# A transformer layer in split float32: the order of additions and splits inside a seven-product pair

## The chip, the cores and the metric

The kernel runs on one core of a Trainium2 chip. The metric is the device time of one execution in microseconds (us), the median of several runs.

## What is computed

One layer works on x of 256 tokens by 2048 channels, all float32, with a norm before and after each part:

```
x = x + 0.5 * rms_norm(swiglu(rms_norm(x), W1_gate_up, W1_down))      # FFN 1, 2048 -> 2 x 5632 -> 2048
p = rms_norm(x) @ W_in                                                 # 2048 -> 6656
y_h = hgrn2 recurrence, forward and backward, 8 heads; y_a = attention, window 128, 8 heads
x = x + rms_norm(concat(y_h, y_a) @ W_out)                             # 2048 -> 2048
x = x + 0.5 * rms_norm(swiglu(rms_norm(x), W2_gate_up, W2_down))      # FFN 2, as FFN 1
```

Nearly all of the work is the products with the weights, 400 MB of which pass once.

## The kernel before

**Split products.** Every float32 matrix is written as h + l: h is the value rounded to the matmul's short float format, l the rest. A product is three matmuls: h with h, h with l, l with h. `split_act` makes the two parts: ScalarE copies the source into h (line 188), and VectorE subtracts h from the source into l (line 189). `split_half(raw, i)` does this for half i of a weight tile `raw` (128 partitions by 2048), so 1024 columns at a time. The weights come from DRAM into `raw` tiles by loads that the SyncE queue (SP) issues in order (line 164); there are three such tiles, for a time a fourth (`raw3`, or `rooms`, the place of X while X is not needed). The h and l tiles come from two pools of five each; a new split waits until TensorE has read the split five before.

**Pairs.** `Blocks` runs a product over pairs u of 128-row blocks of the contraction (256 rows). A plain pair takes 8 products (24 matmuls, `plain`). A seven-product pair (`seven`) takes 7 products (21 matmuls) by a scheme of Strassen's kind: the weight tile has four blocks b11, b12, b21, b22 of 512 columns, and sums of blocks are multiplied with sums of the left side. It needs four kinds of right sides:

- b11 as loaded: a split of 512 columns (`h, l`);
- the lower blocks b21 and b22 as loaded: `lower`, a split of the tile's second half;
- b11 and b22 each plus b12, written over b11 and b12 by one addition of 1024 columns (line 477): `upper`, a split of the first half;
- b22 plus the new b11 (line 481) and b21 plus that (line 483), written over b22 and b21: `last`, a second split of the second half.

So the additions of lines 481 and 483 overwrite what `lower` reads, and the last one must be done before `last`. The seven products are issued in the order b11, `lower` (two), `upper` (two), `last` (two).

**Stages.** `Gated` computes gate and up: 11 groups (g) of 512 columns, each over 8 pairs, of which pairs 1, 3 and 5 are seven-product ones from group 2 on (3 and 5 in group 1, none in group 0). `Pairs` computes the two down projections (11 of 22 pairs by seven products) and the output projection (2 of 8), in two halves of 1024 columns each. At a group's end `fold` (lines 520 to 528) adds the extra products, `units` applies silu and scale (lines 944 and 945), transposes, splits and sums (lines 400 to 404).

**The order of the work.** What each engine runs is in program order on that engine, but the program's order is not the order of the code: outside of stretches marked as manual a scheduler puts every engine's instructions in order by its own estimate of when they will be ready. So a change in the code's order can move instructions on all engines, or be undone.

Of the kernel before, what the change touches and what calls it, by code (L numbers as in the profile page):

```python
# [17 lines left out]
ALU = mybir.AluOpType  # L18
# [19 lines left out]
def hymba_layer_kernel(  # L38
# [25 lines left out]
    nc = tc.nc  # L64
# [11 lines left out]
    def nm(s):  # L76
        uid[0] += 1
        return f"{s}_{uid[0]}"

    def pa():  # L80
        return psum.tile([P, 512], F32, tag="pa", name=nm("pa"))

    def pb():
        return psum.tile([P, 512], F32, tag="pb", name=nm("pb"))
# [59 lines left out]
    def new_raw():  # L144

        raw_places.append(raw_places.pop(0))
        return raw_places[-1]

    def load(src, between=None):
        raw = new_raw()  # L150
        if len(src.shape) == 4:

            dst = raw.rearrange("p (a n b) -> p a n b", a=src.shape[1], n=src.shape[2])
            parts = [(dst[:, a], src[:, a]) for a in range(src.shape[1])]
        else:
            n = src.shape[1]
            dst = raw.rearrange("p (a b) -> p a b", a=n)
            parts = [(dst, src)]
            if n == 2:
                parts = [(dst[:, a], src[:, a]) for a in range(2)]  # L160
        for i, (to, of) in enumerate(parts):
            if i and between:
                between()
            nc.sync.dma_start(to, of)
        return raw
# [14 lines left out]
    def split_half(raw, i, hp=hip, lp=lop):  # L180
        part = raw[:, i * 1024 : (i + 1) * 1024]
        h = hp.tile([P, 1024], F32R, tag="h", name=nm("h"))
        l = lp.tile([P, 1024], F32R, tag="l", name=nm("l"))
        split_act(h, l, part)
        return h, l

    def split_act(hi, lo, src):
        nc.scalar.copy(hi, src)  # L188
        nc.vector.tensor_tensor(lo, src, hi.bitcast(F32), ALU.subtract)  # L189
# [217 lines left out]
    class Blocks:  # L407
# [58 lines left out]
        def seven(self, u, aside=None):  # L466

            self.left_early(u)
            raw = load(self.source(u))
            if aside:  # L470
                aside()
            b11, b12, b21, b22 = (raw[:, i * 512 : (i + 1) * 512] for i in range(4))
            four = raw.rearrange("p (i c) -> p i c", i=4)
            h, l = self.one_block()
            split_act(h, l, b11)

            nc.vector.tensor_tensor(  # L477
                four[:, 0:2], four[:, 0::3], four[:, 1:2].to_broadcast([P, 2, 512]), ALU.add
            )
            lower = split_half(raw, 1)  # L480
            nc.vector.tensor_tensor(b22, b11, b22, ALU.add)  # L481
            upper = split_half(raw, 0)
            nc.vector.tensor_tensor(b21, b22, b21, ALU.add)  # L483
            if aside:
                aside()
            last = split_half(raw, 1)
            if not self.p:
                self.p = [pa(), pa(), pb(), pb()]
            a, w = self.tiles[u], self.left_sums(u)

            def lhs(k, m):
                return [a[:, k, i, m * P : (m + 1) * P] for i in range(2)]

            def summed(j):
                return [w[:, j, i, :] for i in range(2)]

            def rhs(two, n):
                return [x[:, n * 512 : (n + 1) * 512] for x in two]

            for at, left, right in (  # L500
                (("p", 0), lhs(0, 0), (h, l)),
                (("c", 0, 0), lhs(1, 0), rhs(lower, 0)),
                (("c", 0, 1), summed(S4), rhs(lower, 1)),
                (("p", 1), summed(S1), rhs(upper, 0)),
                (("p", 3), summed(S3), rhs(upper, 1)),
                (("p", 2), summed(S2), rhs(last, 1)),
                (("c", 1, 0), lhs(1, 1), rhs(last, 0)),
            ):
                self.three(at, *left, *right)
# [523 lines left out]
    with tc.manual_schedule():  # L1033
# [9 lines left out]
        raw = new_raw()  # L1043
# [561 lines left out]
```

## Time and profile before

| | us |
|---|---|
| median of 3 runs (lowest, highest) | 1855.11 (1854.1, 1856.63) |
| the profiled execution | 1852.71 |
| its span, first to last instruction | 1850.9 |

| engine | busy us | share |
|---|---|---|
| TensorE matmul (PE) | 1831.9 | 99% |
| TensorE weight load (PEld) | 1516.0 | 82% |
| VectorE (DVE) | 1633.6 | 88% |
| ScalarE (ACT) | 1087.2 | 59% |

The granted TensorE clock is 0.999 of full speed on the mean. Weight loads run beside matmuls, and matmuls overlap, so the busy time of TensorE says little on how densely it works; the starts of its instructions do. In rows of the timeline the first number is the start, the second the time taken, both in us; x2 is two instructions merged; a bracket is idle time of the engine ahead of the row and what ended it. In rows of the waits, the total comes first, then how often, then the longest.

### The profile page before, as it was taken

What the parts mean: (1) busy time and instruction counts of PE and PEld (TensorE: products, weight loads), DVE (VectorE), ACT (ScalarE), POOL (GpSimd) and SP (SyncE); (2) the same over time, 40 slices, a digit from 0 to 9 for tenths busy, and PEclk for the clock granted to TensorE, in tenths of its full rate; (3) what the DMA queues carried; (4) which work ended last, traced back from release to release, by engine and by line L of the source; (5) the groups of instructions that cost most, each with busy time, mean ns of one, the idle gap of its engine ahead of it and who ended that gap; (6) DMA issues with size and microseconds to landing.
All of it is one profiled execution on the core that took longest, in us unless ns stands there. A gap on an engine that the chain in (4) does not pass through costs nothing.

```text
span 1850.9 us, 23980 instructions
## 1 busy us (share of the span) xinstructions
PE 1831.9 (99%) x8604; PEld 1516.0 (82%) x8604; DVE 1633.6 (88%) x2076; ACT 1087.2 (59%) x1465; POOL 33.3 (2%) x61
## 2 busy tenths in 40 slices
PE   9999999999999999999999999999999999999998
PEld 7888888888887787888888887888888888888786
DVE  7999999999999998577787798899999999999997
ACT  6555555555655556577677565555555555555563
POOL 1000000000000000000000000000000000000000
PEclk9999999999999999999999999999999999999999
DMA  8566666666877776655565565666666666687774
GB/s 286 191 221 214 205 194 204 206 207 202 291 267 266 242 242 209 217 177 158 168 186 165 182 215 184 205 216 209 211 202 215 219 217 205 218 282 273 242 268 172
DMA packets 192056, 400.45 MB, mean 216 GB/s; under 512 B 11976, under 2 KB 59168, under 8 KB 191168
## 3 DMA queue, kind: packets, MB, share of 16 engines
q1 hardware_dynamic: 188416, 387.24, 63.9%
q0 software_dynamic: 3520, 11.67, 1.6%
q8 instruction: 67, 1.10, 0.2%
q14 instruction: 53, 0.43, 0.1%
HBM read 383.12 MB, written 15.75 MB: 215 GB/s over the span
## 4 chain that ended last, share of the span: by engine, by line
PE 80%; DVE 10%; issue 4%; ACT 3%; DMA 3%; SPq 0%; POOL 0%; ACTq 0%; DVEq 0%; POOLq 0%
PE pa L444 33%; PE pb L444 30%; PE pa L319 8%; DVE l L189 5%; PE pa L324 4%; ACT h L188 2%; DMA raw<-in_w_mix_out_dram 1%; DMA raw<-in_w_ffn_gate_up_dram 1%; PE pa L374 1%; PE pa L373 1%; PE pa L372 1%; DVE raw L477 1%; DVE raw L481 1%; ACT xt L239 0%; PE pa L956 0%
## 5 line engine op out<-in xcount | busy, mean ns | idle before, releaser
L188 ACT CAST h<-raw 128x1024 fp32r<-128x1024 f32 (+1 forms) x691 | 676.8, 1013 | 489.7 <-DVE raw L483 179.2
L189 DVE TENSOR_TENSOR l<-raw,h 128x1024 fp32r<-128x1024 f32 (+1 forms) x691 | 794.4, 1173 | 116.5 <-ACT h L188 83.4
L444 PE MATMUL pa<-h,xt 128*128 128x512 f32 x1176 | 408.7, 393 | 1.5
L444 PE MATMUL pb<-h,xt 128*128 128x512 f32 x1060 | 370.1, 390 | 0.0
L444 PEld LDWEIGHTS pa<-h,xt 128*128 128x128 f32 x1176 | 220.0, 188 | 51.4 <-ACT h L188 7.4
L444 PEld LDWEIGHTS pb<-h,xt 128*128 128x128 f32 x1060 | 198.9, 188 | 42.2 <-DVE pb L528 0.7
L444 PE MATMUL pa<-l,xt 128*128 128x512 f32 x588 | 229.7, 391 | 0.7 <-DVE l L189 0.7
L444 PE MATMUL pb<-l,xt 128*128 128x512 f32 x530 | 206.5, 390 | 0.0
L188 ACT CAST h<-rooms 128x1024 fp32r<-128x1024 f32 x138 | 142.1, 1050 | 57.2 <-DVE rooms L483 40.8
L189 DVE TENSOR_TENSOR l<-rooms,h 128x1024 fp32r<-128x1024 f32 x138 | 165.8, 1219 | 5.3 <-ACT h L188 5.0
L319 PE MATMUL pa<-xt,h 128*128 128x512 f32 x672 | 164.7, 394 | 0.0
L444 PE MATMUL pa<-h,ht 128*128 128x512 f32 x440 | 156.1, 391 | 1.1 <-DVE pa L522 0.9
L444 PE MATMUL pb<-h,ht 128*128 128x512 f32 x440 | 155.8, 390 | 0.2 <-DVE pb L526 0.2
L319 PEld LDWEIGHTS pa<-xt,h 128*128 128x128 f32 x672 | 123.0, 188 | 23.6
L444 PEld LDWEIGHTS pa<-l,xt 128*128 128x128 f32 x588 | 110.5, 188 | 24.8 <-DVE l L189 2.3
L444 PEld LDWEIGHTS pb<-l,xt 128*128 128x128 f32 x530 | 99.5, 188 | 20.6
L477 DVE TENSOR_TENSOR raw<-raw 128x1024 f32<-128x1024 f32 x92 | 112.1, 1218 | 0.4
L444 PEld LDWEIGHTS pa<-h,ht 128*128 128x128 f32 x440 | 82.6, 188 | 20.1 <-DVE pa L525 1.6
L444 PEld LDWEIGHTS pb<-h,ht 128*128 128x128 f32 x440 | 82.6, 188 | 18.2 <-DVE pb L526 1.1
L324 PE MATMUL pa<-xt,l 128*128 128x256 f32 x672 | 91.8, 286 | 0.0
L324 PEld LDWEIGHTS pa<-xt,l 128*128 128x128 f32 x672 | 87.1, 191 | 3.2
L444 PE MATMUL pa<-l,ht 128*128 128x512 f32 x220 | 85.7, 390 | 0.0
(280 smaller groups left out, 2474.4 us busy)
## 6 DMA issues: line engine op xcount, KB each, us to landing
raw<-in_w_ffn_gate_up_dram SPq DMA_DIRECT2D x270, 512.0 KB, 4.9
raw<-in_w_ffn_down_dram SPq DMA_DIRECT2D x132, 512.0 KB, 5.3
raw<-in_w_mix_in_dram SPq DMA_DIRECT2D x52, 1024.0 KB, 5.1
rooms<-in_w_ffn_gate_up_dram SPq DMA_DIRECT2D x80, 512.0 KB, 5.4
rooms<-in_w_ffn_down_dram SPq DMA_DIRECT2D x44, 512.0 KB, 5.1
sp<-ss SPq DMA_DIRECT2D x44, 512.0 KB, 6.5
raw<-in_w_mix_out_dram SPq DMA_DIRECT2D x32, 512.0 KB, 4.8
ss<-rooms POOLq DMA_DIRECT2D x22, 512.0 KB, 5.3
```

What stands on the lines that cost most here:

```text
L188: nc.scalar.copy(hi, src)
L189: nc.vector.tensor_tensor(lo, src, hi.bitcast(F32), ALU.subtract)
L319: nc.tensor.matmul(slot[f], weights(hs, kk, f), xcol(xt, k), start=(k == 0), stop=(k == KT - 1))
L324: nc.tensor.matmul(slot[f][:, 0:T], weights(ls, kk, f), xcol(xt, kh * 8 + kk, 0), start=False, stop=False,)
L372: nc.tensor.matmul(dst, xh, h[:, o : o + n], start=(k == 0), stop=False)
L373: nc.tensor.matmul(dst, xh, l[:, o : o + n], start=False, stop=False)
L374: nc.tensor.matmul(dst, xl, h[:, o : o + n], start=False, stop=(k == KT - 1))
L444: nc.tensor.matmul(self.bank(at), lhs, rhs, start=(n == 1), stop=n in (ends, self.of[at]), skip_group_check=n > ends,)
L477: nc.vector.tensor_tensor(four[:, 0:2], four[:, 0::3], four[:, 1:2].to_broadcast([P, 2, 512]), ALU.add)
L481: nc.vector.tensor_tensor(b22, b11, b22, ALU.add)
```

## The change

In `seven`, the split of the lower blocks as loaded now comes first, directly behind that of b11; then the three additions follow each other; then the other two splits. Nothing is added or removed. The lines behind it move up by one: the three additions are on lines 477, 480 and 481 in the changed kernel.

```
             h, l = self.one_block()
             split_act(h, l, b11)
-
+            lower = split_half(raw, 1)
             nc.vector.tensor_tensor(
                 four[:, 0:2], four[:, 0::3], four[:, 1:2].to_broadcast([P, 2, 512]), ALU.add
             )
-            lower = split_half(raw, 1)
             nc.vector.tensor_tensor(b22, b11, b22, ALU.add)
+            nc.vector.tensor_tensor(b21, b22, b21, ALU.add)
             upper = split_half(raw, 0)
-            nc.vector.tensor_tensor(b21, b22, b21, ALU.add)
             if aside:
                 aside()
             last = split_half(raw, 1)
```

What the scheduler makes of it is not one order for all pairs. In a gate/up group the first seven-product pair keeps the order of before (line 477, both splits, the two other additions, the last split), and the third had the new order before the change already. The second one changes, in groups 2 to 9 of both FFNs; so does the first one of group 1 in the first FFN, and two pairs at the middle of each down projection. On VectorE, in group 3 of the first FFN (groups 4 to 9 read the same), before; the first row is the l of b11, raw_114 the weight tile, l_1452, l_1457 and l_1462 are `lower`, `upper` and `last`, l_1489 the next plain pair's first:

```order
L189 TENSOR_TENSOR l_1447<-raw_114,h_1446 128x512
L189 TENSOR_TENSOR rooms_495<-rooms_495 128x4x128
L477 TENSOR_TENSOR raw_114<-raw_114 128x1024
L189 TENSOR_TENSOR l_1452<-raw_114,h_1451 128x1024
L189 TENSOR_TENSOR l_1457<-raw_114,h_1456 128x1024
L481 TENSOR_TENSOR raw_114<-raw_114 128x512
L483 TENSOR_TENSOR raw_114<-raw_114 128x512
L189 TENSOR_TENSOR l_1462<-raw_114,h_1461 128x1024
L189 TENSOR_TENSOR l_1489<-raw_112,h_1488 128x1024
```

The same place in the changed kernel, where `lower`, `upper` and `last` are l_1451, l_1458 and l_1462:

```order
L189 TENSOR_TENSOR l_1447<-raw_114,h_1446 128x512
L189 TENSOR_TENSOR l_1451<-raw_114,h_1450 128x1024
L189 TENSOR_TENSOR rooms_495<-rooms_495 128x4x128
L477 TENSOR_TENSOR raw_114<-raw_114 128x1024
L480 TENSOR_TENSOR raw_114<-raw_114 128x512
L481 TENSOR_TENSOR raw_114<-raw_114 128x512
L189 TENSOR_TENSOR l_1458<-raw_114,h_1457 128x1024
L189 TENSOR_TENSOR l_1462<-raw_114,h_1461 128x1024
L189 TENSOR_TENSOR l_1489<-raw_112,h_1488 128x1024
```

The split of `lower` moved ahead of line 477, that of `upper` behind the three additions, next to `last`. Ahead of these rows, the first split of the plain pair from the spare room moved from behind line 400 to in front of it, and on ScalarE its h moved ahead of the copy of line 964.

On TensorE at the end of the same pair, before; h_1461 and l_1462 are `last`, h_1488 and l_1489 the next plain pair's:

```order
L444 MATMUL pb_1387<-h_1461,xs_521 128x512
L444 MATMUL pb_1304<-h_1461,xt_126 128x512
L444 MATMUL pa_1302<-h_1488,xt_127 128x512
L444 MATMUL pa_1303<-h_1488,xt_127 128x512
L444 MATMUL pb_1387<-l_1462,xs_521 128x512
L444 MATMUL pb_1387<-h_1461,xs_521 128x512
L444 MATMUL pb_1304<-l_1462,xt_126 128x512
```

And in the changed kernel:

```order
L444 MATMUL pb_1387<-h_1461,xs_521 128x512
L444 MATMUL pb_1387<-l_1462,xs_521 128x512
L444 MATMUL pb_1387<-h_1461,xs_521 128x512
L444 MATMUL pb_1304<-h_1461,xt_126 128x512
L444 MATMUL pb_1304<-l_1462,xt_126 128x512
L444 MATMUL pb_1304<-h_1461,xt_126 128x512
L444 MATMUL pa_1302<-h_1488,xt_127 128x512
```

The matmuls with h, which had been put ahead of those with l_1462, went back behind them: each product's three matmuls now stand together.

In the output projection, VectorE at the first seven-product pair, before (raw_112 is the weight tile, l_9094 and l_9099 are `lower` and `upper`; ya, g, ot and yh belong to the heads that are being finished):

```order
L477 TENSOR_TENSOR raw_112<-raw_112 128x1024
L189 TENSOR_TENSOR ya_8996<-pb_8991,ya_8996 128x2x256
L189 TENSOR_TENSOR l_9094<-raw_112,h_9093 128x1024
L1381 TENSOR_TENSOR g_8977<-g_8977,sg_8983 128x512
L481 TENSOR_TENSOR raw_112<-raw_112 128x512
L1384 SCALAR_TENSOR_TENSOR ot_8697<-ot_8697,cols,g_8977 128x256 x2
L189 TENSOR_TENSOR l_9099<-raw_112,h_9098 128x1024
L189 TENSOR_TENSOR yh_8988<-ot_8697,yh_8988 128x2x256
L483 TENSOR_TENSOR raw_112<-raw_112 128x512
```

And in the changed kernel, `lower` and `upper` being l_9093 and l_9100:

```order
L189 TENSOR_TENSOR l_9093<-raw_112,h_9092 128x1024
L189 TENSOR_TENSOR ya_8996<-pb_8991,ya_8996 128x2x256
L477 TENSOR_TENSOR raw_112<-raw_112 128x1024
L1380 TENSOR_TENSOR g_8977<-g_8977,sg_8983 128x512
L480 TENSOR_TENSOR raw_112<-raw_112 128x512
L1383 SCALAR_TENSOR_TENSOR ot_8697<-ot_8697,cols,g_8977 128x256 x2
L481 TENSOR_TENSOR raw_112<-raw_112 128x512
L189 TENSOR_TENSOR l_9100<-raw_112,h_9099 128x1024
L189 TENSOR_TENSOR yh_8988<-ot_8697,yh_8988 128x2x256
```

The last addition moved ahead of the split of `upper`, and line 477 changed places with the split of `lower`. Further on in this stage, a split that had stood ahead of an addition of the next pair moved behind it.

More of the change, by code (lines that the diff above doesn't have):

```diff
@@ L475, in seven @@
             split_act(h, l, b11)
+            lower = split_half(raw, 1)
             nc.vector.tensor_tensor(
@@ L479, in seven @@
             )
-            lower = split_half(raw, 1)
             nc.vector.tensor_tensor(b22, b11, b22, ALU.add)
+            nc.vector.tensor_tensor(b21, b22, b21, ALU.add)
             upper = split_half(raw, 0)
-            nc.vector.tensor_tensor(b21, b22, b21, ALU.add)
             if aside:
```

## The prediction

> **What bounds the kernel now.** I read the page's busy times first, then the stretches of one repeated group, then every start of TensorE inside it, and only then the queues that feed it.
>
> ```profile
> PE 1831.9 (99%) x8604; PEld 1516.0 (82%) x8604; DVE 1633.6 (88%) x2076; ACT 1087.2 (59%) x1465; POOL 33.3 (2%) x61
> 163.67:206.63 42.96, 42.84 (x192) 35.03 (x191) 39.94 (x48) 24.17 (x30) 0.53 (x1) 1.00 0.64 209
> ```
>
> The first row is the whole span: TensorE looks full, VectorE nearly so. The second is one gate/up group (span; then PE, PEld, DVE, ACT and POOL busy with their counts; granted clock; DMA): 42.96 us for 192 matmuls, with VectorE busy for 39.94 of it. Busy matmuls overlap, so whether TensorE is at its pace must be read from starts. Here is a stretch that runs freely (the third seven-product pair of a group) and one that does not (behind the second).
>
> ```profile
> 214.55 0.39 PE L444 MATMUL pa<-l,xt 128*128 128x512 f32 x1
> ...
> 217.27 0.39 PE L444 MATMUL pb<-l,xs 128*128 128x512 f32 x1
> 205.71 0.39 PE L444 MATMUL pb<-h,xs 128*128 128x512 f32 x1
> ...
> 206.63 0.40 PE L444 MATMUL pb<-h,xt 128*128 128x512 f32 x1
> 207.15 0.74 PE L444 MATMUL pa<-h,xt 128*128 128x512 f32 x2
> 207.73 0.40 PE L444 MATMUL pb<-l,xs 128*128 128x512 f32 x1
> ```
>
> From 214.55 to 217.27 lie 12 steps: 0.227 us each, which is TensorE's pace for 512 columns. From 206.63 to 207.73 are three steps, 1.10 us where 0.68 would do: 0.42 us lost, in one group. The waits say for whom, and how often (the first row is of 110 to 450 us, the next two of 1190 to 1560 us):
>
> ```profile
> PEld pa L444 <- ACT h L188: 4.5, 8, 0.6
> PEld pa L444 <- ACT h L188: 2.9, 6, 0.6
> PEld pb L444 <- DVE l L189: 1.4, 3, 0.5
> 1248.37 0.39 PE L444 MATMUL pb<-h,xt 128*128 128x512 f32 x1
> ...
> 1249.11 0.40 PE L444 MATMUL pb<-h,xs 128*128 128x512 f32 x1
> ```
>
> Eight groups of the first FFN lose it, 0.56 us of weight-load wait each. In the second FFN four lose the same; two wait (2.9 - 4 x 0.56) / 2 = 0.33 us, and of the three that wait for l, one is in the group numbered 1, whose order the change leaves alone; the other two look like 1248.37: two steps in 0.74 us, 0.29 lost. So TensorE is the bound, and what can be won is its bubbles alone. Why the split comes late is on VectorE and ScalarE:
>
> ```profile
> 198.84 0.68 DVE L189 TENSOR_TENSOR l<-raw,h 128x512 fp32r<-128x512 f32 x1
> 199.44 0.68 DVE L189 TENSOR_TENSOR rooms<-rooms 128x512 fp32r<-128x512 f32 x1
> 200.05 1.22 DVE L477 TENSOR_TENSOR raw<-raw 128x1024 f32<-128x1024 f32 x1
> 201.18 2.49 DVE L189 TENSOR_TENSOR l<-raw,h 128x1024 fp32r<-128x1024 f32 x2
> 203.58 0.69 DVE L481 TENSOR_TENSOR raw<-raw 128x512 f32<-128x512 f32 x1
> 204.30 0.69 DVE L483 TENSOR_TENSOR raw<-raw 128x512 f32<-128x512 f32 x1
> 206.19 5.23 DVE L189 TENSOR_TENSOR l<-raw,h 128x1024 fp32r<-128x1024 f32 x5 [1.20 <-ACT h L188]
> 196.73 1.57 ACT L188 CAST h<-raw 128x512 fp32r<-128x512 f32 x2
> 201.35 1.06 ACT L188 CAST h<-raw 128x1024 fp32r<-128x1024 f32 x1 [2.53 <-DVE raw L477]
> 205.11 4.42 ACT L188 CAST h<-raw 128x1024 fp32r<-128x1024 f32 x5 [2.70 <-DVE raw L483]
> ```
>
> The last addition (L483) ends at 204.99; only then can ScalarE round the last half (205.11 to 206.16), while VectorE idles for 1.20 us and then needs 1.23 us for its l. Behind it on both engines stand the splits of the next plain pair, and TensorE, out of work at 206.63, waits for the first h of that pair.
>
> **The change part by part.** No instruction is added or removed; what counts is the order that the program gets. It changes little: the third pair of each group already has the new order before, the first keeps the old one after. The second pair of groups 2 to 9 of both FFNs changes on VectorE, ScalarE and TensorE, so 16 places; then one pair in group 1 of the first FFN, two in each down projection, and the output projection.
>
> *A gate/up group.* What lies ahead of 198.84 keeps its sum (a split of the spare room changes places with small operations). From there, by the durations above, each start about 0.09 before the end of the one in front where it doesn't depend on it, as 199.44 against 199.52: l of b11 198.84 to 199.52; l of the lower half 199.44 to 200.66 (its h is the second of the two of ACT 196.73, done by 198.30: no wait); the split into rooms to 201.25; L477 201.17 to 202.39; the next two additions depend on it, each 0.03 behind: to 203.11 and 203.83; l of the upper half 203.74 to 204.96 (its h runs on ScalarE from 202.4 to 203.5); l of the last half 204.87 to 206.09 (its h from 203.9 to 204.9). The 1.20 us are covered by the upper l. TensorE needs the upper l for the second matmul of its set: the row 205.71 starts the set after it, three steps earlier is 205.03, so 205.26. It is there 0.3 us before that. It needs the last half's h at 206.39 and its l at 206.62: 1.5 and 0.5 us before. The next pair's h is done at 205.9 (needed about 207.75) and its l at 207.2 (needed about 207.98). So the whole 0.42 goes. That three additions in a row followed by two splits starve nobody is seen in the third pair, with the same rows already:
>
> ```profile
> 211.34 1.22 DVE L477 TENSOR_TENSOR raw<-raw 128x1024 f32<-128x1024 f32 x1
> 212.59 0.69 DVE L481 TENSOR_TENSOR raw<-raw 128x512 f32<-128x512 f32 x1
> 213.32 0.69 DVE L483 TENSOR_TENSOR raw<-raw 128x512 f32<-128x512 f32 x1
> 213.93 2.50 DVE L189 TENSOR_TENSOR l<-raw,h 128x1024 fp32r<-128x1024 f32 x2
> ```
>
> No bracket stands there, and TensorE's 12 free steps above are this pair's. Sum: 8 x 0.42 = 3.4 in the first FFN; 4 x 0.42 + 2 x 0.29 + 2 x 0.25 (0.33 scaled by 0.42 / 0.56) = 2.8 in the second; 6.2 us. Bounds: nothing, if the wait returns elsewhere (0), and 16 x 0.42 = 6.7. VectorE loses 16 x 1.2 us of waiting as well, which gives nothing by itself: it is paced by TensorE's end of the group.
>
> A rule for judging this: the Trainium skill, Perfetto Trace Analysis, section Optimization Strategy, says that the same gap repeating on the engine that should be saturated can mean that there is not enough room for the next tile. By it the bubble would stay and the sum would be 0; it is among the rivals below. The row ACT 205.11 goes against it: that engine waits for an addition.
>
> *Queues.* The raw tile's first half is now freed by the upper l (204.96) and not by L481 (204.27), so its next load is issued 0.7 us later by SP, in order, and the loads behind it too; the second half is free at 206.09 and not 207.42. That load feeds a split some 14 us later and takes about 5 us: hidden, unless all of about 9 us of cover are gone.
>
> *The down projections, and group 1.* In each down projection an L477 and the l behind it change places, twice, in a stretch where VectorE runs without a gap; what follows ends at the same time. In group 1 of the first FFN the same is done once, and TensorE waits for nothing there. I take 0, between -0.3 and +0.3.
>
> *The output projection*, first half. Here the cover is missing:
>
> ```profile
> 1055.17 1.21 DVE L189 TENSOR_TENSOR l<-raw,h 128x1024 fp32r<-128x1024 f32 x1
> 1056.41 1.28 SPq L164 DMA_DIRECT2D raw<-in_w_mix_out_dram  x3
> 1062.62 3.90 ACT L188 CAST h<-raw 128x1024 fp32r<-128x1024 f32 x4 [6.72 <-DMA raw<-in_w_mix_out_dram]
> 1064.67 0.50 PE L444 MATMUL pb<-h,sp 128*128 128x512 f32 x1 [0.81 <-ACT h L188]
> 1101.67 1.23 DVE L189 TENSOR_TENSOR l<-raw,h 128x1024 fp32r<-128x1024 f32 x1 [0.50 <-ACT h L188]
> 1103.97 1.23 DVE L189 TENSOR_TENSOR l<-raw,h 128x1024 fp32r<-128x1024 f32 x1 [1.07 <-ACT h L188]
> 1121.17 0.50 PE L444 MATMUL pa<-h,ya 128*128 128x512 f32 x1 [0.91 <-DVE pa L525]
> ```
>
> SP's three loads wait behind the upper l at 1055.17; the last addition (0.68) now stands in front of that l, so loads, ScalarE's h and TensorE's wait at 1064.67 come up to 0.7 us later. In the new order TensorE has two matmuls of the next pair (0.45) ahead of the one that waits: I take +0.2, between 0 and +0.7. Later the split that waited 1.07 us (1103.97) no longer stands ahead of an addition, so the chain to L525, for which TensorE waits 0.91 at 1121.17, can be up to 1.1 us earlier: I take -0.4, between -1.1 and +0.7 (if the later loads carry through). Net -0.2.
>
> Sum: -6.2 - 0.2 = -6.4 us. The profiled execution took 1852.7 us (span 1850.9), so 1846.3 for such a one; it lies 2.4 below the median of the runs, 1855.1, against which the forecast is 1848.7.
>
> **The rivals.**
>
> *Only part of it comes.* The margin of the upper l is 0.3 us, and TensorE's order changes with it. If half of the places keep a bubble of 0.2 to 0.4 us, the gain is about 3: 1852. For it: the bubbles differ from group to group (0.42, 0.29, 0.25). Against: VectorE's rows from 163 to 450 us repeat exactly.
>
> *Nothing comes.* Were the bubble a lack of h and l buffers, order would not help: 1855.1. For it: there are only five of each, and ScalarE waits for them elsewhere:
>
> ```profile
> ACT h L188 <- PE pb L444: 106.5, 75, 3.8
> ```
>
> Against: at 205.11 the wait is for L483.
>
> *VectorE is the bound.* Then the 1.20 us of each of the 16 places would come off: 19.2, so 1835.9. For it: 88% busy. Against: the pace of 0.227. The Trainium skill, Perfetto Trace Analysis, section Identifying the Most-Contended Engine, says that matmul busy time tells little and weight-load time more; by that, TensorE at 82% would have room and VectorE would be fuller. The even starts decide against it here.
>
> *Slower: the wait moves ahead of the additions.* The lower l now comes directly behind that of b11. If its h were late by as much as the 1.20 us that the last one waits today, the upper l would end at 206.16, 0.90 after it is needed; with 0.11 that a matmul behind a wait loses (1064.67 shows 0.50 for 0.39), less the 0.42 won, 0.59 us are lost in each of 16 places: +9.4, so 1864.5. It decides at a delay of 0.3 + 0.42 - 0.11 = 0.6 us. For it: ScalarE now does one more split of the spare room before a copy ahead of it. Against: that h ended 1.1 us before it would be read.
>
> **How the numbers follow.** The forecast 1848.7 has 0.68, the part gain 0.15, nothing 0.08, VectorE 0.03, slower 0.06. 0.2% is 3.7 us, about what a measurement can tell: faster is the forecast, VectorE and a little of the part gain (0.73), the same the rest of that and nothing (0.20), slower 0.07. The range reaches down by 0.5 in the FFNs, 1.3 in the output projection and 0.9 for the spread of the runs (1854.1 to 1856.6), to 1846.0; up over the part gain and its spread, to 1853.6; it leaves out nothing, slower, VectorE and a little more.
>
> **What would show it.** Right: groups of 42.5 us instead of 42.96; no wait of 1.20 in front of the second pair's last l; a single such wait per group left (the first pair's); the waits of the weight load for h gone between 110 and 450 us. Wrong: a bracket in front of the lower or upper l, a new wait of TensorE for an l, or groups that stay at 42.96 because another queue sets the period; a larger wait at 1064 than 1.2 us would put the output projection's term wrong.

## The result, and the profile after

The changed kernel took 1844.97 us in the median (six runs, 1843.91 to 1847.07); the kernel before, run beside it, 1854.61 (six runs, 1852.23 to 1856.63). The ratio is 0.995, with a 95% interval of 0.9938 to 0.9963: 9.6 us less by the medians, 9.3 by the ratio, 6.9 to 11.5 by the interval. The forecast was 1848.7 with a range down to 1846.0: the direction came as forecast, and the time is 1.0 us below the range. One execution of a kernel below (2015.96 us, at a granted clock of 0.85) is left out of its median.

The profiled execution took 1845.13 us (span 1843.4), 7.6 less than the one of before. First the page's busy times after, then the stretch that answers to the group shown before (it begins and ends at the same matmuls, the 721st and the 912th in TensorE's order), the next one, and one in the second FFN (span; then PE, PEld, DVE, ACT, POOL busy with their counts; clock; DMA share; GB/s):

```profile
PE 1826.4 (99%) x8604; PEld 1518.3 (82%) x8604; DVE 1637.5 (89%) x2076; ACT 1098.5 (60%) x1465; POOL 33.2 (2%) x61
163.41:206.00 42.59, 42.59 (x192) 35.10 (x191) 40.60 (x48) 24.86 (x30) 0.53 (x1) 1.00 0.64 215
206.00:248.60 42.60, 42.60 (x193) 35.10 (x191) 40.21 (x48) 24.86 (x30) 0.53 (x1) 1.00 0.63 210
1456.77:1499.36 42.59, 42.59 (x192) 35.11 (x191) 40.20 (x48) 24.86 (x30) 0.53 (x1) 1.00 0.64 210
```

A group takes 42.59 us where it took 42.96. VectorE's busy time did not fall; it only stands closer. Now VectorE and ScalarE at the second seven-product pair (start, length, engine, line, operation; in brackets the idle time before it and what ended it), then TensorE's first and last row of the stretch behind it:

```profile
199.12 1.23 DVE L477 TENSOR_TENSOR raw<-raw 128x1024 f32<-128x1024 f32 x1
200.38 0.69 DVE L480 TENSOR_TENSOR raw<-raw 128x512 f32<-128x512 f32 x1
201.11 0.69 DVE L481 TENSOR_TENSOR raw<-raw 128x512 f32<-128x512 f32 x1
201.72 6.57 DVE L189 TENSOR_TENSOR l<-raw,h 128x1024 fp32r<-128x1024 f32 x6
200.44 1.06 ACT L188 CAST h<-raw 128x1024 fp32r<-128x1024 f32 x1 [2.91 <-DVE raw L477]
201.89 3.47 ACT L188 CAST h<-raw 128x1024 fp32r<-128x1024 f32 x4 [0.40 <-DVE raw L481]
204.64 0.39 PE L444 MATMUL pa<-l,xs 128*128 128x512 f32 x1
...
206.91 0.39 PE L444 MATMUL pb<-h,xt 128*128 128x512 f32 x1
```

The bracket of 1.20 us in front of the last split is gone: six splits stand in one row from 201.72, because ScalarE's h of the last half runs while VectorE makes the upper l. From 204.64 to 206.91 TensorE makes 10 steps in 2.27 us, its pace of 0.227, where it had lost 0.42. The weight load's waits for h between 110 and 450 us (4.5 us before) are no longer listed; this is the largest that is (total, count, longest):

```profile
PEld pb L444 <- issue: 2.3, 7, 0.3
```

What remains in a group stands behind its first seven-product pair, which kept its order:

```profile
191.43 1.22 DVE L189 TENSOR_TENSOR l<-raw,h 128x1024 fp32r<-128x1024 f32 x1 [1.20 <-ACT h L188]
195.99 0.69 DVE L189 TENSOR_TENSOR ht<-pb,ht 128x512 fp32r<-128x512 f32 x1
196.49 0.39 PE L444 MATMUL pa<-h,xt 128*128 128x512 f32 x1
196.82 0.47 PE L444 MATMUL pb<-h,xs 128*128 128x512 f32 x1
197.12 0.39 PE L444 MATMUL pb<-l,xs 128*128 128x512 f32 x1
```

VectorE waits its 1.20 us there still, and TensorE takes 0.33 and 0.30 for two steps: 0.18 lost (before it was 0.11 at this place, so 0.07 of the gain went here). Last, the two places of the output projection that the prediction priced:

```profile
1060.30 0.73 PE L444 MATMUL pa<-h,ya 128*128 128x512 f32 x2 [0.29 <-ACT h L188]
1061.24 0.50 PE L444 MATMUL pb<-h,sp 128*128 128x512 f32 x1 [0.21 <-ACT h L188]
1098.92 0.69 DVE L480 TENSOR_TENSOR raw<-raw 128x512 f32<-128x512 f32 x1
1100.67 0.69 DVE L481 TENSOR_TENSOR raw<-raw 128x512 f32<-128x512 f32 x1
1104.57 5.77 DVE L189 TENSOR_TENSOR l<-raw,h 128x1024 fp32r<-128x1024 f32 x5 [0.95 <-ACT h L188]
1115.87 0.39 PE L444 MATMUL pa<-h,ya 128*128 128x512 f32 x1
1116.43 0.50 PE L444 MATMUL pa<-h,ya 128*128 128x512 f32 x1 [0.18 <-DVE pa L524]
```

In the first half the one wait of 0.81 for an h has become two, 0.29 and 0.21. In the second half the wait for line 525 (524 now) fell from 0.91 to 0.18: VectorE still waits 0.95 for an h, but both additions stand ahead of that wait, no longer behind it.

### The profile page after: what moved, and what is told of

Its sections match the earlier page's. It is cut to its first block, busy times and chain, and to the rows that moved or that the text cites. A ratio compares the mean times of both kernels' runs of the same rounds, so it can differ in the third digit from the quotient of the medians.

```text
span 1843.4 us, 23959 instructions
## 1 busy us (share of the span) xinstructions
PE 1826.4 (99%) x8604; PEld 1518.3 (82%) x8604; DVE 1637.5 (89%) x2076; ACT 1098.5 (60%) x1465; POOL 33.2 (2%) x61
## 4 chain that ended last, share of the span: by engine, by line
PE 80%; DVE 11%; issue 3%; DMA 3%; ACT 3%; POOL 0%; SPq 0%; DVEq 0%; ACTq 0%; POOLq 0%
PE pa L444 32%; PE pb L444 30%; PE pa L319 8%; DVE l L189 5%; PE pa L324 4%; ACT h L188 2%; DMA raw<-in_w_ffn_gate_up_dram 1%; DMA raw<-in_w_mix_out_dram 1%; PE pa L373 1%; PE pa L374 1%; PE pa L372 1%; DVE raw L477 1%; DVE raw L481 1%; DVE raw L480 1%; DMA raw<-in_w_ffn_down_dram 0%
```

## The experiments

The question is where 9.6 us come from when the working gave 6.4. Theory: the gate/up groups give what their bubbles say, and the rest is other places and the difference between executions. Rivals: a part taken at nothing (the down projections) or at 0.2 us (the output projection) gives more; or VectorE is the bound. Differences from the kernel of before are worked out from the ratio in this section, and those of the medians are named as such.

**The kernel of before, again.** Its edit is none.

> The kernel before, run once more, to tell which TensorE bubbles return and which come by chance. Theory 'chance': the 1.1 us wait for line 522 in the first down projection (594.77 in the first profile) hangs on one load's landing and is missing or of another size here, the 0.42 us bubbles of the gate/up groups are there again; median within 0.2% of before. Rival 'all of it repeats': the same bubbles to 0.05 us everywhere, the 1.1 us wait too.

1855.51 us (11 runs, 1852.43 to 1857.0); ratio to 28 runs of before, which lie between 1851.68 and 1859.42, 1.0006 [0.9997, 1.0015]. The same program spreads over 7.7 us. The bubbles of the gate/up groups are there again; the idle time in front of the matmul that waits for line 522, 0.95 us in the first profile, is 0.17 here.

**Only the gate/up groups.** The changed order where the object is `Gated`, the old one elsewhere:

```diff
+            if isinstance(self, Gated):
+                lower = split_half(raw, 1)
+                # the addition of line 477, then b22, b21
+                upper = split_half(raw, 0)
+            else:
+                # as before
```

> The new order in the gate/up groups alone, the old one in the down and output projections. Theory 'the groups carry it': 16 groups go from about 42.95 to 42.60 us, 5 to 6 us less in all, ratio about 0.997; what the whole change has beyond that is missing. Rival 'the rest carries as much': the groups bring 5 us but the whole change brings 9 to 10, so 4 us must show in the other two kernels.

1848.24 us, ratio 0.9967 [0.9954, 0.998]: -6.1 us (-3.7 to -8.5), and -5.6 by the medians. The groups have the after's 42.58 us.

**Only the down projections**, with `if isinstance(self, Pairs) and self.stored`:

> The new order in the two down projections alone. Theory 'nothing there': within 1 us of before, the groups stay at 42.96 us. Rival: 1.5 to 2.5 us less, with the waits for lines 522, 525 and 526 (0.2 to 1.1 us each) smaller.

1853.73 us, ratio 0.9997 [0.9988, 1.0006]. Nothing that can be measured (-2.2 to +1.1 us).

**Only the output projection**, with `if isinstance(self, Pairs) and not self.stored`:

> The new order in the output projection alone. Theory of the prediction: the wait near 1064 grows by 0 to 0.7 us and the one near 1121 shrinks by up to 1.1 us, 0 to 1 us less in all. Rival 'the queue loses more than it wins': up to 0.7 us more.

1853.68 us, ratio 0.9994 [0.9985, 1.0003]: -1.1 us (-2.8 to +0.6), and -0.2 by the medians. By itself undecided; its waits below decide it. The three parts add to 7.8 us, where the whole change gave 9.3 by the same measure.

**The changed kernel, again.**

> The changed kernel as it is, once more. It came out 2.4 us below the forecast's 6.4 us of gain (9.3 instead of 6.4). Theory: the gate/up groups give 5.5 us in every execution, the rest is the difference of waits that hang on when a load lands and vary from execution to execution; then this run lies between 1845 and 1848.5, its groups at 42.6 us, and waits of 0.3 to 1.1 us come back in the down projections (about 590 us, for L522) or in the output projection's second half (about 1116 us). Rival: the change takes the wait for L522 away for good, 1.1 us; then it is absent here too, in both down projections, and the time is 1845 again.

1846.8 us (five runs, 1845.61 to 1848.46) against 1854.71 of before: ratio 0.9957 [0.9945, 0.997], -8.0 us (7.9 by the medians). Its groups take 42.59 and 42.60, as in the first profile. The wait for line 522 (521 now) at the end of the down projection's first run, 0.95 us in the first profile of before and gone in the first one after, is back. The first row is of the first profile after, the second of this one, at the same matmul:

```profile
591.36 0.47 PE L444 MATMUL pa<-h,ht 128*128 128x512 f32 x1
592.92 0.47 PE L444 MATMUL pa<-h,ht 128*128 128x512 f32 x1 [0.92 <-DVE pa L521]
```

ScalarE shows what it hangs on, a load for which it waits 1.1 us longer in the second execution than in the first:

```profile
585.45 0.62 ACT L188 CAST ha<-raw 128x512 fp32r<-128x512 f32 x1 [1.11 <-DMA raw<-in_w_ffn_down_dram]
587.00 0.62 ACT L188 CAST ha<-raw 128x512 fp32r<-128x512 f32 x1 [2.25 <-DMA raw<-in_w_ffn_down_dram]
```

So that wait goes and comes with the execution, under one and the same order; it belongs to the difference of the two first profiles, not to what the change gives. The two executions of the changed kernel differ by 3.3 us, and by the starts of the same matmuls 1.0 of it lies in the first down projection and 2.0 in the second.

**The first move alone** (the lower split first; `b21` still added behind the upper split), and **the second alone** (three additions together; the lower split still behind the first of them):

```diff
 # first move alone                       # second move alone
+lower = split_half(raw, 1)
 (addition of line 477)                   (addition of line 477)
-lower = split_half(raw, 1)                lower = split_half(raw, 1)
 (addition of b22)                        (addition of b22)
 upper = split_half(raw, 0)              -upper = split_half(raw, 0)
 (addition of b21)                        (addition of b21)
                                         +upper = split_half(raw, 0)
```

> Only the first move: the lower blocks as loaded are split first, the addition of b21 stays behind the upper split in the source. Theory: the scheduler that sets VectorE's order takes it as leave to put all three additions ahead of the upper split in the second pair of a group, so the 1.20 us wait goes, groups take 42.6 us, total 1845 to 1848.5. Rival: both moves are needed, the second pair keeps the wait, groups 42.96, total 1853 to 1856.

> Only the second move: the lower split stays behind the first addition, the three additions stand together ahead of the upper split in the source. Theory: this leaves the second pair of a group as before the change (upper split between the additions, 1.20 us wait of VectorE, 0.42 us of TensorE), groups 42.96 us, total 1853 to 1856. Rival: it is the additions standing together that count, whatever the place of the lower split; then 1846 to 1849.

1847.84 us, ratio 0.9963 [0.9949, 0.9977], and 1853.09 us, ratio 0.9995 [0.9986, 1.0004]. One group of each:

```profile
163.59:206.17 42.58, 42.58 (x193) 35.10 (x192) 40.59 (x48) 24.89 (x30) 0.53 (x1) 1.00 0.65 216
163.76:206.74 42.98, 42.84 (x193) 35.02 (x191) 39.97 (x48) 24.22 (x30) 0.53 (x1) 1.00 0.64 209
```

The first move alone carries the groups' whole gain, though in the source it leaves the additions apart: the scheduler puts them together in the second pair. The second move, which in the source puts them together, leaves the groups as they were. What was written and what VectorE got differ. The two kernels also divide the rest: the first has the changed order in the groups and down projections and the old one in the output projection, the second the reverse. So eight profiles have the changed order in the output projection and five the old one (the later experiments included). TensorE waits there for additions into pa at two places, where `fold` adds up the first half and where it adds up the second. The idle time in front of the waiting matmul, in us:

| order | first half, 1079 to 1085 us | second half, 1116 to 1123 us |
|---|---|---|
| old | before 0, again_before 0.73, gated_only 0.26, down_only 0.61, lower_first 0.91 | before 0.91, again_before 1.05, gated_only 1.10, down_only 2.41, lower_first 0.63 |
| changed | none in any of the eight | after 0.18, again_after 0.24, adds_first 0.31, out_only 0.61, fixed_all 0.31, extra_dve, fixed_groups and plain_between none |

In the mean the second half's wait falls from 1.2 to 0.2 us, and the first half's from 0.5 to nothing. The first half's was not in the working: the profile that the prediction was made from is the only one of its order without it. First TensorE and VectorE there in again_before, then VectorE in the changed kernel:

```profile
1084.35 0.50 PE L444 MATMUL pa<-h,yh 128*128 128x512 f32 x1 [0.73 <-DVE pa L525]
1078.93 1.23 DVE L189 TENSOR_TENSOR l<-raw,h 128x1024 fp32r<-128x1024 f32 x1 [1.53 <-ACT h L188]
1080.08 0.69 DVE L522 TENSOR_TENSOR pa<-pa,y 128x512 f32<-128x512 f32 x1
1069.56 4.63 DVE L189 TENSOR_TENSOR l<-raw,h 128x1024 fp32r<-128x1024 f32 x4 [0.57 <-ACT h L188]
1074.71 0.69 DVE L521 TENSOR_TENSOR pa<-pa,y 128x512 f32<-128x512 f32 x1
```

In the old order a split that waits for its h stands right ahead of the addition of line 522; in the changed one (line 521 there) no such wait stands among these additions. Added up over both halves the two orders do not overlap: 1.7 us in the mean against about 0.2, a gain of 1.5. What makes the second half's wait longer is again a load, here ScalarE's h of one of the last halves in the first profile of before and in down_only:

```profile
1116.73 1.05 ACT L188 CAST h<-raw 128x1024 fp32r<-128x1024 f32 x1 [1.03 <-DMA raw<-in_w_mix_out_dram]
1118.71 1.05 ACT L188 CAST h<-raw 128x1024 fp32r<-128x1024 f32 x1 [2.58 <-DMA raw<-in_w_mix_out_dram]
```

And SP's queue came out in another order. Before, a load of the next stage went ahead of the fourth of these loads (first three rows); after, the four go out together (last row):

```profile
1098.37 3.15 SPq L164 DMA_DIRECT2D raw<-in_w_mix_out_dram  x3
1105.22 0.56 SPq L164 DMA_DIRECT2D raw<-in_w_ffn_gate_up_dram  x1
1106.96 0.34 SPq L164 DMA_DIRECT2D raw<-in_w_mix_out_dram  x1
1094.75 6.36 SPq L164 DMA_DIRECT2D raw<-in_w_mix_out_dram  x4
```

How much of the 1.5 us comes from the earlier loads and how much from the additions' place on VectorE was not separated.

**More work for VectorE.** In each group's second pair, half of the last l is computed twice:

```diff
             last = split_half(raw, 1)
+            if isinstance(self, Gated) and u == 3:
+                nc.vector.tensor_tensor(last[1][:, 0:512], b21, last[0][:, 0:512].bitcast(F32), ALU.subtract)
```

> The changed kernel, with half of the last l of each group's second pair computed a second time: 0.6 us more of VectorE in each of 20 places, 12 us in all, nothing else. Theory (TensorE bounds, VectorE has slack behind this place: the l is needed about 0.7 us after it is ready): groups 42.6 to 42.75 us, total at most 2.5 us above the changed kernel, 1845 to 1848.5. Rival (VectorE, 89% busy, bounds the groups): groups 43.2 us, total 12 us above, 1857. Half of it, 6 us, would say that only part of the groups has the slack.

```profile
207.26 0.68 DVE L487 TENSOR_TENSOR l<-raw,h 128x512 fp32r<-128x512 f32 x1
164.51:207.31 42.80, 42.80 (x192) 35.02 (x191) 40.85 (x50) 24.62 (x31) 0.53 (x1) 1.00 0.64 211
1458.68:1501.26 42.58, 42.58 (x193) 35.10 (x191) 40.72 (x49) 24.87 (x30) 0.53 (x1) 1.00 0.63 209
```

1848.0 us (five runs, 1846.36 to 1848.71), 1.2 more than the changed kernel beside it for about 12 us of added VectorE work (20 operations, 0.60 us each from start to start). Early groups grew by up to 0.2, a little more than expected, late ones not at all. VectorE at 89% is not the bound; at this place it had room for most of one small operation.

**The same order in the first pair too.** VectorE's order written out inside the seven-product pairs of the groups, and in a second kernel in all such pairs:

```diff
+            with tc.manual_schedule(engines={mybir.EngineType.DVE}) if isinstance(self, Gated) else ExitStack():
                 lower = split_half(raw, 1)
                 ...
                 upper = split_half(raw, 0)
```

> The changed kernel, with VectorE's order from the lower split to the upper split written out for the scheduler in every seven-product pair of the gate/up groups. That gives the first pair of a group the order that the change gave to the second alone (three additions, then the upper and the last split). In the changed kernel the first pair keeps VectorE's wait of 1.20 us for the last half's h, and TensorE then loses 98 + 80 ns some 5 us later. Theory: it is the same mechanism, so VectorE's wait goes and TensorE's 0.18 us with it in 16 groups: groups of 42.4 us instead of 42.6, 2.9 us in all, 1843 where the changed kernel takes 1846. Rival: those 0.18 us hang on the order of small operations between the pairs (the unit's turn and sums), which stand there still; groups 42.6, 1846. A third way: the written order puts the splits of the first pair behind operations that wait for TensorE's end of the group, and groups grow, above 1847.

> The same written order in every seven-product pair, those of both down projections and of the output projection too. Theory: VectorE runs without a gap where the down projections lose time on TensorE (1.4 us at 621 us), so the order can't help there; within 1 us of the kernel with the order written for the groups alone. Rival: the scheduler's own interleaving of two pairs hides ScalarE's delay there and a written order loses it: 2 to 6 us longer, in stretches 500 to 700 and 1620 to 1780 us.

The groups' version: 1848.14 us, ratio 0.9971 [0.996, 0.9982]. The first row is a group's stretch, the second the weight load's waits between 110 and 450 us, the rest VectorE at the first pair:

```profile
163.51:206.17 42.66, 42.66 (x192) 35.10 (x191) 40.25 (x48) 24.95 (x30) 0.53 (x1) 1.00 0.64 210
PEld pb L444 <- DVE ht L189: 2.9, 7, 0.4
189.78 0.69 DVE L482 TENSOR_TENSOR raw<-raw 128x512 f32<-128x512 f32 x1
190.38 2.50 DVE L189 TENSOR_TENSOR l<-raw,h 128x1024 fp32r<-128x1024 f32 x2
194.88 0.68 DVE L189 TENSOR_TENSOR ht<-pb,ht 128x512 fp32r<-128x512 f32 x1
```

VectorE's 1.20 us wait went, as in the second pair, and the group became 0.07 longer. TensorE's loss behind the first pair is a wait for the split of `ht`, which frees the bank pb of the transposes. That split is 1.1 us earlier than in the changed kernel (194.88 for 195.99), but the scheduler moved the matmuls into that bank forward as well, by six steps (32.1 us into the group for 33.4). So a wait of VectorE of the same length and cause was worth 0.42 us at one pair and nothing at the other. With the order written out everywhere: 1850.82 us (eleven runs), ratio 0.9986 [0.9978, 0.9995], 2.7 more than the groups' version: the rival. Between 490 and 530 us, the start of a down projection, where the changed kernel lists no wait, TensorE has two new ones:

```profile
PE pa L444 <- DVE l L189: 0.9, 1, 0.9
PE pb L444 <- DVE l L189: 0.6, 1, 0.6
```

**A plain pair put between.** In the second run of each down projection:

```diff
-                [1, 0, 3, 2, 4, 5, 6, 7, 8, 14, 9, ...
+                [1, 0, 3, 2, 5, 4, 6, 7, 8, 14, 9, ...
```

> The changed kernel, with one plain pair moved between two seven-product pairs at the start of the second run of each down projection (order 1, 0, 3, 2, 5, 4, 6, 7 in place of 1, 0, 3, 2, 4, 5, 6, 7). There TensorE waits 1.37 us for an l in both down projections, while VectorE is busy without a gap. Theory: VectorE is the bound there, locally (a seven-product pair costs it about 7.5 us against 4.8 of TensorE, a plain pair 2.4 against 5.4), so the plain pair ahead covers the wait: 1.4 us less in each, 2.7 in all, 1843 where the changed kernel takes 1846. Rival: the shortage only moves to the next two seven-product pairs in a row, some 15 us later: 1846.

1849.03 us, ratio 0.9972 [0.9961, 0.9984]: no gain over the changed kernel. TensorE's waits for an l between 500 and 760 us, in the changed kernel and in this one:

```profile
PE pb L444 <- DVE l L189: 1.2, 1, 1.2
PE pb L444 <- DVE l L189: 1.1, 2, 0.5
```

The wait of 1.2 us at 621 is gone and two of half its size came later: the rival. Nothing tried here beats the changed kernel.

## Why the prediction was right, and where it was wrong

*The bound and the place: right.* TensorE's starts decided, not its or VectorE's busy share. The 1.20 us of VectorE covered a TensorE bubble, and nothing of VectorE's own saving came through. VectorE is not the bound: 12 us of extra VectorE work cost 1.2. By the Trainium skill, Perfetto Trace Analysis, section Identifying the Most-Contended Engine, TensorE's headroom is judged by weight-load time and not by matmul time; here that is 82%, which had put the bound at VectorE. Nor was it a lack of buffers: the bubble went by order alone, with the same buffers. The Trainium skill, Perfetto Trace Analysis, section Optimization Strategy, says that a repeating gap can mean too little room for the next tile; by that the bubble would have stayed. One thing stays open: ScalarE's and TensorE's orders changed together with VectorE's, and no run separates them.

*The gate/up groups: 6.2 predicted, 5.7 measured.* By the starts of the same matmuls in the two first profiles, from ahead of group 2 into the start of the down projection, the first FFN lost 3.2 us (3.4 predicted) and the second 2.6 (2.8). Four more profiles with the changed groups (again_after, gated_only, lower_first, plain_between) give 5.6 to 6.1 against the first profile of before. The term was about 0.4 too large because only the bubble was counted: behind the first pair a further 0.07 was lost, and the period fell by 0.37, not by 0.42. A part of this came back at the end of group 10, where TensorE lost about 0.2 before and nothing after. The kernel with only this part measured 6.1.

*The down projections and group 1: 0, not contradicted, but wrong in its bounds.* The order does nothing there that can be measured (0.9997). But the bounds of 0.3 are not what one execution can show: the wait for line 522 alone is 0.95, 0.17, 0 and 0.92 us in the two profiles of before and the two after, by the execution.

*The output projection: the term that failed.* It was taken at -0.2; by TensorE's starts, in the mean of the five profiles with the old order and the eight with the changed one, it is -1.6. The wait at 1064 was right: +0.2 predicted, +0.15 measured (nothing between the two first profiles: 0.97 us at the first wait and 0.18 just behind it before, 1.13 over five steps after). But the first half's fold was put at nothing, because the one profile that was read has no wait there, and it gave -0.7. The second half was taken at -0.4 and gave -1.05, just inside its bound of -1.1. The place was the one named, and the additions do stand ahead of the waiting split now, but the size was read from one execution, in which the wait was 0.9; the old order shows 0.6 to 2.4. And SP's queue, which the prediction followed in the first half alone, came out better in the second.

*The base and the range: the other step that failed.* Groups 5.7 and output projection 1.6 make 7.3; from the base of 1855.1 that is 1847.8, which the range holds. The first median lies 2.8 below it, the second 1.0. Of the 2.8, 0.5 is the base, 1854.61 in the runs beside it. Each against its own runs of before, the comparisons gave 9.6 and 7.9; the intervals, 6.9 to 11.5 and 5.6 to 10.2, hold about that sum. So 0.6 to 2.3 us of the medians are not placed in any stage. The difference of the two first profiles, 7.6 us, can be placed by the starts of the same matmuls: groups 5.7, first down projection 1.9, output projection 0.9, second down projection 0.3, while the stages between the first down projection and the output projection gave 1.2 back. The down projections vary that much between two executions of the changed kernel, so their share is luck. What is shown is that the medians of six and five runs of one kernel differ by 1.8 (1844.97 and 1846.8), and that runs of before spread over 7.7 us. The range had allowed 0.9 for this, from three runs, and had carried the sum from one profiled execution over to their median as if both lost the same at every wait; that allowance was too small.

*The rivals.* Part gain, nothing, VectorE, slower: none came. The lower l behind that of b11 did not wait, and TensorE lists no wait for it.

## What to carry to other kernels

Price a reorder by the bubbles of the engine that sets the pace, place by place: two waits of 1.20 us on VectorE with one cause were worth 0.42 us and nothing. Look at what the scheduler made of an edit before trusting the source: in the groups one of two moves did all the work, and it was not the one that reads like it. And where a wait hangs on transfers, take its size from several executions, or give it bounds as wide as the runs spread.

## What was not expected of the hardware

A matmul that follows one that waited loses time too. In the changed kernel's down projection:

```profile
621.04 0.61 PE L444 MATMUL pb<-h,sp 128*128 128x512 f32 x2
622.87 0.50 PE L444 MATMUL pb<-l,sp 128*128 128x512 f32 x1 [1.21 <-DVE l L189]
623.21 0.40 PE L444 MATMUL pb<-h,sp 128*128 128x512 f32 x1
```

The matmul that waited starts 1.60 us after the one in front of it (which is the second of the first row, at 621.27), 1.37 more than the pace of 0.227, for a bracket of 1.21: the bracket counts from the end of the matmul in front, as the profile has it. And the step behind it is 0.34 us instead of 0.227, so 0.11 more is lost. Behind the other waits of the down and output projections the step is 0.33 to 0.34 too, except behind the one for line 522, where it is 0.31 with a wait and without. So by starts a wait there costs mostly about 0.27 more than its bracket. And with the granted clock at 0.998 or 0.999 in every profile here, ScalarE's wait for a single load still moved by 1.1 us between two executions of one kernel (its rows at 585 and 587 us above), and by 1.6 between two kernels with the same order at that place (1116 and 1118 us), part of the 7.7 us by which runs of one program differ.
